# One token tile's merged activations turned by DMA transpose instead of TensorE, in a hybrid GLA/HGRN2 layer

## The chip, the cores and the metric

The kernel runs on one core of a Trainium2 chip. The metric is the device time of one execution in microseconds, as the median of several runs. The profile is of one further execution on the same kind of chip.

## The reference

One layer of a decoder trunk on 256 tokens of width 2048, all in float32. It has three parts: a SwiGLU half-step, a token mixer, and a second SwiGLU half-step. Each normalizes its input (RMSNorm) and normalizes its output again before it is added to the residual `h`. Cut to what matters here:

```python
f1 = swiglu(rms_norm(h, ...), ffn1_w_gate, ffn1_w_up, ffn1_w_down)      # D_FF = 5504
h = h + 0.5 * rms_norm(f1, ffn1_post_norm)
proj = rms_norm(h, mix_pre_norm) @ w_in                                 # eleven slices
o_gla, o_hgrn = ...                    # two causal gated recurrences, (256, 1024) each
merged = (sigmoid(z_gla + b0) * (o_gla @ w_branch_gla)
          + sigmoid(z_hgrn + b1) * (o_hgrn @ w_branch_hgrn))            # (256, 2048)
h = h + rms_norm(merged @ w_out, mix_post_norm)
f2 = swiglu(rms_norm(h, ...), ffn2_w_gate, ffn2_w_up, ffn2_w_down)
h = h + 0.5 * rms_norm(f2, ffn2_post_norm)
```

The change touches the way from `merged` to its product with `w_out`.

## The kernel before, in words

The 256 tokens are two token tiles (`NT` = 2) of 128 rows. A matrix product runs over row tiles of 128 input features and column blocks of 512 (`CB`). The weights are streamed from HBM in chunks of 128x1024 floats (`raw`). To keep float32 accuracy, every operand is split into a high part (`hi`, a copy by ScalarE, line 159) and a low part (`lo`, the difference, by VectorE, line 161). `mm3` (lines 165 to 167) then makes three matmuls: hi times hi, lo times hi, hi times lo. The split weights lie in a ring of five slots (`RING`); a new chunk can be split only when TensorE has finished with a slot. Some pairs of row tiles are done with seven block products in place of eight (`Blocks.seven`, lines 273 to 310); these need sums of weight blocks (`wsum`, split into `wsumh` and `wsuml`) and sums of activation blocks (`four_sums`).

A product's left operand must be turned, with features on the partitions. `to_T` (line 454) does this for a 128x512 block: four transposes on TensorE into a PSUM bank (`transpose4`, line 403), then ScalarE and VectorE split the bank into the `hi` and `lo` tiles, and `x[2][t]` is set to the number of row tiles that are ready. There is a second way, used by the feed-forward halves (`finish`, lines 678 to 689): `halved` (line 418) copies the block on ScalarE so that the low and the high 16 bits of all its floats lie apart, `turn` (line 426) issues a DMA transpose of the 16-bit data from ScalarE's queue, and `joined` (line 432) copies the turned halves on ScalarE back into floats.

The merge works like this. `ms[n][t]` holds the gated GLA branch and `szs[n][t]` the HGRN2 gate, for the column blocks n = 0 to 3. For each n, `gemm_block` multiplies by `w_branch_hgrn` (8 row tiles, 48 matmuls), and for each tile t `merge` (lines 1224 to 1232) is spawned: VectorE multiplies the product by the gate (line 1226) and adds the other branch (line 1227); then the block is turned by `to_T` into `mT`, and then the residual, which had been put away in DRAM (`away`), is loaded back over `ms` (line 1232, on ScalarE's queue).

After the merge `in_halves` multiplies `mT` by `w_out`, over two halves of the columns. The first half takes the row tiles in the order `OUT[0]`: 0, 1, the seven-product step of unit 1 (row tiles 2 and 3), 4, 5, that of unit 3 (row tiles 6 and 7), then 8 to 15. Column block n of the merge is row tiles 4n to 4n + 3. `sums_of(u)` makes the sums of unit u from `mT` of both tiles. `lhs_of` makes the program wait until the row tile that it wants has been written.

Order: small jobs are Python generators in a list (`Side`). Each `yield` ends a turn, and the gemm loops give all jobs a turn (`side.pump`) after every weight chunk, and twice in a seven-product step. This sets the order in the program. The framework then builds each engine's queue from the program and from its own estimate of when an instruction's inputs are ready; an engine works through its queue in that order. So the place of an instruction in the program is a rank and not a time: the trace has instructions of the merge and of the first sums well ahead of where the turns would put them.

Of the kernel before, what the change touches and what calls it, by code (L numbers as in the profile page):

```python
# [94 lines left out]
def kernel(ctx: ExitStack, tc: tile.TileContext, a: dict, out: bass.AP):  # L95
    nc = tc.nc
# [14 lines left out]
    def nm(s):  # L111
        uid[0] += 1
        return f"{s}_{uid[0]}"

    def ps_tile(s="ps"):
        return psum.tile([P, CB], F32, tag="ps", name=nm(s))
# [3 lines left out]
    away = [[dram.tile([P, CB], F32, name=f"away{t}_{n}") for n in range(4)] for t in range(NT)]  # L120
# [37 lines left out]
    def split_into(hi, lo, src):  # L158
        last[0] = nc.scalar.activation(hi, src, AF.Copy)  # L159
        with tc.issue_after(first_ops.pop().ins) if first_ops else nullcontext():  # L160
            nc.vector.tensor_tensor(lo, src, hi.bitcast(F32), op=ALU.subtract)  # L161
# [241 lines left out]
    def transpose4(dst_ps, src, n=4):  # L403
        for i in range(n):
            end = nc.tensor.transpose(dst_ps[:, i * P:(i + 1) * P], src[:, i * P:(i + 1) * P],  # L405
                                      ident)
        return end

    def tiles4(x):
        return x.rearrange("p (k c) -> p k c", c=P)  # L410

    def move(eng, dst, src):
        if eng is nc.scalar:
            nc.scalar.activation(dst, src, AF.Copy)
        else:
            eng.tensor_copy(dst, src)

    def halved(src, halves, eng=nc.scalar):

        w = src.shape[-1]  # L420
        halves = halves.bitcast(U16)[:, :2 * w]
        move(eng, halves.rearrange("p (h f) -> p h f", h=2),
             src.bitcast(U16).rearrange("p (f h) -> p h f", h=2))
        return halves

    def turn(halves):
        turned = work.tile([P, 8, P], U16, tag="tmp", name=nm("turned"), bufs=3)
        turned = turned[:, :halves.shape[-1] // P, :]
        nc.scalar.dma_start_transpose(turned, halves)
        return turned  # L430

    def joined(dst, turned, eng=nc.scalar):

        move(eng, dst.bitcast(U16).rearrange("p j (k h) -> p h j k", h=2),
             turned.rearrange("p (h j) k -> p h j k", h=2))

    def new_xT():
        x = [None] * NT, [None] * NT, [0] * NT
        for t in range(NT):
            alloc_xT(x, t)  # L440
        return x
# [12 lines left out]
    def to_T(x, t, n, src, col=None):  # L454


        ps = ps_tile()
        transpose4(ps, src)
        sl = slice(4 * n, 4 * n + 4)
        v = tiles4(ps)  # L460
        if col is not None:
            v = tiles4(work.tile([P, CB], F32, tag="tmp", name=nm("u"), bufs=3))
            nc.vector.tensor_tensor(v, tiles4(ps), col[:, sl].unsqueeze(2).broadcast_to([P, 4, P]),
                                    op=ALU.mult)
        split_into(x[0][t][:, sl, :], x[1][t][:, sl, :], v)
        x[2][t] = 4 * n + 4
# [295 lines left out]
    def mixer(x, rs, ready, following):  # L762
        xl = lhs_of(x)
        w_in = a["w_in"]
        with ExitStack() as mctx:
# [5 lines left out]
            def blk(s, dt=F32):  # L771
                return b2.tile([P, CB], dt, tag="b", name=nm(s), bufs=33)
# [449 lines left out]
            mT = new_xT()  # L1222

            def merge(t, n, b):
                s, m = szs[n][t], ms[n][t]
                nc.vector.tensor_tensor(s, b, s, op=ALU.mult)
                nc.vector.tensor_tensor(s, m, s, op=ALU.add)
                yield
                to_T(mT, t, n, s)
                for _ in range(6):  # L1230
                    yield
                nc.scalar.dma_start(m, away[t][n])

            side.until(lambda: not side.heavy)
            for n in range(4):
                b = gemm_block(a["w_branch_hgrn"], n * CB, CB, o_lhs("h"), nkt=8, ready=ready)
                ready = ()
                for t in range(NT):
                    side.spawn(merge(t, n, b[t]))
# [118 lines left out]
```

## Time and profile before

| | |
|---|---|
| median of 3 runs | 2058.8 us (2058.33 to 2060.32) |
| the profiled execution | 2058.24 us |
| its span, first to last instruction | 2056.4 us |
| mean granted TensorE clock | 0.999 |
| TensorE matmuls | 10319 |
| transposes of merged tiles, line 405 | 32, from 1253.1 to 1289.4 us |
| products with `w_branch_hgrn` | about 1239 to 1286 us |
| first half of the product with `w_out` | begins at 1285.87 us |
| ScalarE busy, whole span | 1317.2 us (64%) |
| DMA transposes (feed-forward halves) | 44 |

How to read it: a row of the trace has the start in microseconds, the duration, the engine, the line of the kernel, the operation, the output and input tiles, and at its end, in brackets, how long the engine had been idle before it and what ended this. `ACTq` and `SPq` are the queues' own instructions, such as the issue of a DMA. A row of waits has the waiting engine and line, what it waited for, the total in microseconds, the number of times and the longest. A row for a source line has three durations in nanoseconds: least, median and longest. The chain of waits goes back from the last instruction to what released it, and so on to the start.

### The profile page before, as it was taken

The numbers are of one execution on the slowest core, as the hardware profiler recorded it, in microseconds if no ns is written. First come the engines' busy times: TensorE is split into PE (matmuls) and PEld (weight loads), VectorE is DVE, ScalarE is ACT, GpSimd is POOL, SyncE is SP. The second block draws the span as 40 slices with busy tenths as digits, with TensorE's granted clock in tenths as the row PEclk, the third lists the DMA queues.
The fourth block names the chain that finished last, engine by engine and source line by source line (L and its number), as shares of the span: only waits on it lengthen the run. The fifth ranks groups of instructions, "written<-read, shape, count | busy, mean of one in ns | idle before, by whom it ended". The sixth has DMA issues, their size and how long they took to land.

```text
span 2056.4 us, 29076 instructions
## 1 busy us (share of the span) xinstructions
PE 2044.6 (99%) x10319; PEld 1699.8 (83%) x10319; DVE 1898.8 (92%) x2235; ACT 1317.2 (64%) x1726; POOL 42.4 (2%) x87
## 2 busy tenths in 40 slices
PE   9999999999999999999999999999999999999998
PEld 9888888888888888878888888888888888888886
DVE  8999999998999889989999898888999999999897
ACT  7666666666666576577655565556666666666663
POOL 1000000000000100000000000010000000000000
PEclk9999999999999999999999999999999999999999
DMA  8777677676757567556566566657767767776664
GB/s 258 223 215 230 203 217 224 212 225 206 233 182 235 157 199 224 158 177 191 167 201 191 180 219 217 219 156 211 235 203 220 223 214 208 224 236 201 205 194 146
DMA packets 247834, 423.51 MB, mean 206 GB/s; under 512 B 63668, under 2 KB 72055, under 8 KB 247688
## 3 DMA queue, kind: packets, MB, share of 16 engines
q1 hardware_dynamic: 196624, 401.80, 61.9%
q10 hardware_dynamic: 51064, 19.84, 4.6%
q8 instruction: 81, 1.33, 0.3%
q14 instruction: 65, 0.53, 0.1%
HBM read 406.11 MB, written 4.19 MB: 200 GB/s over the span
## 4 chain that ended last, share of the span: by engine, by line
PE 94%; DVE 3%; ACT 1%; issue 1%; DMA 1%; POOL 0%; DVEq 0%; POOLq 0%; ACTq 0%
PE c L165 22%; PE c L167 22%; PE c L166 22%; PE p L167 6%; PE p L165 6%; PE p L166 6%; PE mm L167 3%; PE mm L165 3%; PE mm L166 2%; PE ps L405 1%; DVE wlo L161 1%; DVE h L543 1%; PE ps L881 0%; DVE held L161 0%; DMA raw<-in_ffn_w_gate_dram 0%
## 5 line engine op out<-in xcount | busy, mean ns | idle before, releaser
L159 ACT ACTIVATE whi<-raw 128x1024 fp32r<-128x1024 f32 (+3 forms) x490 | 496.2, 1026 | 213.6 <-PE c L166 100.1
L161 DVE TENSOR_TENSOR wlo<-raw,whi 128x1024 fp32r<-128x1024 f32 (+3 forms) x490 | 573.7, 1184 | 44.1 <-ACT whi L159 42.2
L165 PE MATMUL c<-whi,xhi 128*128 128x512 f32 (+1 forms) x1358 | 529.2, 390 | 0.0
L166 PE MATMUL c<-whi,xlo 128*128 128x512 f32 (+1 forms) x1358 | 525.6, 387 | 0.0
L167 PE MATMUL c<-wlo,xhi 128*128 128x512 f32 (+1 forms) x1358 | 525.5, 387 | 0.0
L251 DVE TENSOR_TENSOR wlo<-raw,whi 128x1024 fp32r<-128x1024 f32 x264 | 314.4, 1219 | 20.4 <-ACT whi L290 15.4
L165 PEld LDWEIGHTS c<-whi,xhi 128*128 128x128 f32 x1358 | 254.9, 188 | 51.1 <-ACT xhi L502 0.6
L167 PEld LDWEIGHTS c<-wlo,xhi 128*128 128x128 f32 x1358 | 254.9, 188 | 50.8
L166 PEld LDWEIGHTS c<-whi,xlo 128*128 128x128 f32 x1358 | 255.0, 188 | 49.4
L290 ACT ACTIVATE whi<-raw 128x1024 fp32r<-128x1024 f32 x132 | 139.4, 1056 | 192.0 <-DVE raw L251 88.9
L251 DVE TENSOR_TENSOR wsuml<-wsum,wsumh 128x1536 fp32r<-128x1536 f32 x132 | 231.3, 1752 | 7.4 <-ACT wsumh L292 7.3
L165 PE MATMUL c<-whi,hkhi 128*128 128x512 f32 x542 | 210.9, 389 | 0.0
L167 PE MATMUL c<-wlo,hkhi 128*128 128x512 f32 x542 | 210.8, 389 | 0.0
L166 PE MATMUL c<-whi,hklo 128*128 128x512 f32 x542 | 210.8, 389 | 0.0
L288 ACT ACTIVATE wsumh<-wsum 128x1024 fp32r<-128x1024 f32 x132 | 139.0, 1053 | 87.9 <-DVE wsum L251 45.3
L286 ACT ACTIVATE whi<-raw 128x1024 fp32r<-128x1024 f32 x132 | 139.0, 1053 | 83.1 <-PE c L166 57.5
L251 DVE TENSOR_TENSOR wsum<-raw,raw 128x1024 f32<-128x1024 f32 x132 | 161.1, 1220 | 21.7 <-DMA raw<-in_ffn_w_down_dram 14.0
L167 PEld LDWEIGHTS c<-wlo,hkhi 128*128 128x128 f32 x542 | 101.7, 188 | 21.3
L166 PEld LDWEIGHTS c<-whi,hklo 128*128 128x128 f32 x542 | 101.7, 188 | 21.2
L165 PEld LDWEIGHTS c<-whi,hkhi 128*128 128x128 f32 x542 | 101.7, 188 | 20.9
L251 DVE TENSOR_TENSOR c<-c,psum 128x512 f32<-128x512 f32 x143 | 94.8, 693 | 11.5 <-PE c L167 11.2
L251 DVE TENSOR_TENSOR psum<-psum,p 128x512 f32<-128x512 f32 (+1 forms) x108 | 92.8, 859 | 2.3 <-ACT psum L318 0.6
(342 smaller groups left out, 3030.1 us busy)
## 6 DMA issues: line engine op xcount, KB each, us to landing
raw<-in_ffn_w_down_dram SPq DMA_DIRECT2D x120, 512.0 KB, 4.8
raw<-in_w_in_dram SPq DMA_DIRECT2D x104, 512.0 KB, 4.4
raw<-in_ffn_w_gate_dram SPq DMA_DIRECT2D x90, 512.0 KB, 4.8
raw<-in_ffn_w_up_dram SPq DMA_DIRECT2D x90, 512.0 KB, 3.7
raw<-in_ffn_w_gate_dram SPq DMA_DIRECT2D x140, 256.0 KB, 3.9
raw<-in_ffn_w_up_dram SPq DMA_DIRECT2D x140, 256.0 KB, 4.1
raw<-in_w_in_dram SPq DMA_DIRECT2D x128, 256.0 KB, 3.6
raw<-in_ffn_w_down_dram SPq DMA_DIRECT2D x104, 256.0 KB, 3.9
```

The lines of the kernel that those rows point to most:

```text
L159: last[0] = nc.scalar.activation(hi, src, AF.Copy)
L161: nc.vector.tensor_tensor(lo, src, hi.bitcast(F32), op=ALU.subtract)
L165: nc.tensor.matmul(ps, lhsT=xhi, rhs=whi, start=start, stop=False)
L166: nc.tensor.matmul(ps, lhsT=xlo, rhs=whi, start=False, stop=False)
L167: nc.tensor.matmul(ps, lhsT=xhi, rhs=wlo, start=False, stop=stop)
L251: return nc.vector.tensor_tensor(o, x, y, op=op)
L286: nc.scalar.activation(ahi, ra, AF.Copy)
L288: nc.scalar.activation(hi[:, 0:2, :], wsum[:, 0:2, :], AF.Copy)
L290: nc.scalar.activation(bhi, rb, AF.Copy)
L405: end = nc.tensor.transpose(dst_ps[:, i * P:(i + 1) * P], src[:, i * P:(i + 1) * P], ident)
L543: nc.vector.scalar_tensor_tensor(h[t][n], acc[t][n], r1, h[t][n], op0=ALU.mult, op1=ALU.add)
```

## The change

Only `merge` is touched. The second tile (t = 1) stays on TensorE, with twelve turns instead of six before its residual load. The first tile (t = 0) goes the feed-forward halves' way: the merged block's halves are copied by ScalarE into a new tile from the pool of 33 shared tiles, turned by DMA, and, eight turns later, joined by ScalarE over the merged block; a turn later they are split into `mT` from SBUF instead of from PSUM, `mT`'s count is set, and a turn after that the residual is loaded.

```diff
                 nc.vector.tensor_tensor(s, b, s, op=ALU.mult)
                 nc.vector.tensor_tensor(s, m, s, op=ALU.add)
                 yield
-                to_T(mT, t, n, s)
-                for _ in range(6):
+                if t:
+                    to_T(mT, t, n, s)
+                    for _ in range(12):
+                        yield
+                    nc.scalar.dma_start(m, away[t][n])
+                    return
+                halves = halved(s, blk("halves"))
+                yield
+                turned = turn(halves)
+                for _ in range(8):
                     yield
+                joined(tiles4(s), turned)
+                yield
+                sl = slice(4 * n, 4 * n + 4)
+                split_into(mT[0][t][:, sl, :], mT[1][t][:, sl, :], tiles4(s))
+                mT[2][t] = 4 * n + 4
+                yield
                 nc.scalar.dma_start(m, away[t][n])
```

The helpers that it calls:

```python
    def halved(src, halves, eng=nc.scalar):
        w = src.shape[-1]
        halves = halves.bitcast(U16)[:, :2 * w]
        move(eng, halves.rearrange("p (h f) -> p h f", h=2),
             src.bitcast(U16).rearrange("p (f h) -> p h f", h=2))
        return halves

    def turn(halves):
        turned = work.tile([P, 8, P], U16, tag="tmp", name=nm("turned"), bufs=3)
        turned = turned[:, :halves.shape[-1] // P, :]
        nc.scalar.dma_start_transpose(turned, halves)
        return turned

    def joined(dst, turned, eng=nc.scalar):
        move(eng, dst.bitcast(U16).rearrange("p j (k h) -> p h j k", h=2),
             turned.rearrange("p (h j) k -> p h j k", h=2))
```

## The prediction, made before the changed kernel ran

> **What bounds the kernel now.** I read the page's first part and its chain first, to see which engine sets the end; then TensorE's waits, to see whether anything ever holds it up; then the chain, the groups and the timeline of the stage from 1240 to 1320 us, where the changed code runs.
>
> ```profile
> PE 2044.6 (99%) x10319; PEld 1699.8 (83%) x10319; DVE 1898.8 (92%) x2235; ACT 1317.2 (64%) x1726; POOL 42.4 (2%) x87
> PE 94%; DVE 3%; ACT 1%; issue 1%; DMA 1%; POOL 0%; DVEq 0%; POOLq 0%; ACTq 0%
> PE ps L1298 <- POOL idle L1293: 1.3, 1, 1.3
> PE mm L167 <- DVE wlo L161: 0.8, 1, 0.8
> PE ps L941 <- ACT state L951: 0.4, 1, 0.4
> PE c L167 <- DVE held L161: 0.3, 1, 0.3
> PE ps L405 <- DVE h L543: 0.2, 1, 0.2
> ```
>
> TensorE (PE) works through 99% of the span and is 94% of the chain that ended last. All waits that the trace lists for it come to 1.3 + 0.8 + 0.4 + 0.3 + 0.2 = 3.0 us in 2056.4, none of them at the merge. So the end moves by what TensorE is given or spared, unless an edit makes it wait where it now does not. Two questions remain: how much of its time the removed transposes are, and whether the longer way of a tile by DMA can make it wait.
>
> **The removed transposes.** The 32 transposes of the merge stand in the chain of waits as six pieces, each long until the next matmul takes over:
>
> ```profile
> 1253.26 0.87 PE ps L405 x8
> 1265.04 0.44 PE ps L405 x4
> 1266.18 0.44 PE ps L405 x4
> 1276.85 0.44 PE ps L405 x4
> 1278.43 0.53 PE ps L405 x4
> 1288.75 0.87 PE ps L405 x8
> L405 PE MATMUL ps<-ident,sz x32: 270/272/329, 1253.1 to 1289.4; 128*128 128x128 f32 x32
> ```
>
> A piece of 8 is both tiles' four transposes of one column block (blocks 0 and 3), a piece of 4 is one tile's. Together they are 0.87 + 0.44 + 0.44 + 0.44 + 0.53 + 0.87 = 3.59 us. The change keeps the second tile's, four pieces of 4: 4 x 0.44 = 1.76 us. Spared: 3.59 - 1.76 = **1.83 us**, or 0.11 us for each of 16 transposes. The row of the transposes gives 0.272 us for each, but that is an instruction's own duration, and neighbours overlap; by it the sum would be 16 x 0.272 = 4.35 us. I take the chain's pieces, which are what the next matmul waits for, and keep 4.35 as the far end.
>
> The Trainium skill (TensorE: Matmul & The Clock Gate, Part 4: PE-mode transpose) gives about 275 ns for a transpose inside a kernel; an estimate from that page would be 16 x 0.275 = 4.4 us. The trace agrees on the duration, at 0.272 us, and not on what it costs the stream.
>
> **What is added to ScalarE (ACT) and its queue.** The feed-forward halves turn tiles of this size by the same helpers, so the trace has the prices:
>
> ```profile
> L414 ACT ACTIVATE halves<-silu x44: 825/1043/1060, 44.5 to 1825.5; 128x1024 uint16<-128x1024 uint16 x40, 128x768 uint16<-128x768 uint16 x4
> L414 ACT ACTIVATE hT<-turned x44: 1048/1360/1384, 51.6 to 1841.1; 128x1024 uint16<-128x1024 uint16 x40, 128x768 uint16<-128x768 uint16 x4
> L429 ACTq DMA_TRANSPOSE turned<-halves x44: 1233/1250/2367, 45.4 to 1826.9; - x44
>   ACT hT L414: 10.9, 10
> DMA to landing us min/median/max: 3.1/4.8/7.9
> 1254.08 1.06 ACT L159 ACTIVATE xhi<-ps 128x512 fp32r<-128x512 f32 x2
> 1260.41 0.62 ACT L159 ACTIVATE ms<-sums 128x512 fp32r<-128x512 f32 x1
> 1255.36 1.28 DVE L161 TENSOR_TENSOR xlo<-ps,xhi 128x512 fp32r<-128x512 f32 x2
> 1262.29 0.68 DVE L161 TENSOR_TENSOR ms<-sums,ms 128x512 fp32r<-128x512 f32 x1
> 1277.00:1289.00 12.00, 12.00 (x59) 9.81 (x58) 11.96 (x17) 6.05 (x8) 0.00 (x0) 1.00 0.67 196
> 1297.00:1307.00 10.00, 10.00 (x46) 8.28 (x45) 9.47 (x9) 6.96 (x9) 0.00 (x0) 1.00 0.65 206
> ```
>
> Per block of the first tile: copying the halves 1.04 us, issuing the DMA transpose 1.25 us, joining 1.36 us, 3.65 us in all and 14.6 us for four blocks. The split itself stays: its ScalarE half took 0.53 us from PSUM (1.06 for two) and 0.62 from SBUF on a tile of the same size, its VectorE (DVE) half 0.64 and 0.68, so it costs at most 0.1 us more. In the first window (after the length: TensorE, weight load, VectorE, ScalarE) ScalarE is busy 6.05 us of 12, about one block's pace, which leaves 6 us for 3.65. I cost this at nothing, because ScalarE fits it into idle time. The transposes' bytes go beside the weights, and DMA is 0.65 to 0.67 busy there (the last column but one); TensorE never waited for a weight in this stage, so I cost them at nothing too.
>
> The cover is the ring of split weights. The wait rows below show ScalarE idle until TensorE lets a ring slot go:
>
> ```profile
> 1253.12 1.06 ACT L159 ACTIVATE whi<-raw 128x1024 fp32r<-128x1024 f32 x1 [1.66 <-PE mm L166]
> 1292.22 1.06 ACT L286 ACTIVATE whi<-raw 128x1024 fp32r<-128x1024 f32 x1 [1.58 <-PE c L166]
> 1293.45 0.63 ACT L159 ACTIVATE ms<-sums 128x512 fp32r<-128x512 f32 x1 [0.16 <-DVE sums L214]
> 1296.96 1.06 ACT L290 ACTIVATE whi<-raw 128x1024 fp32r<-128x1024 f32 x1 [2.88 <-PE c L166]
> 1297.93 1.04 ACT L288 ACTIVATE wsumh<-wsum 128x1024 fp32r<-128x1024 f32 x1
> 1298.88 0.62 ACT L292 ACTIVATE wsumh<-wsum 128x512 fp32r<-128x512 f32 x1
> 1299.71 1.75 DVE L251 TENSOR_TENSOR wsuml<-wsum,wsumh 128x1536 fp32r<-128x1536 f32 x1
> 1305.57 0.39 PE L167 MATMUL p<-wsuml,ms 128*128 128x512 f32 x1
> ```
>
> A step of the gemm is 12 matmuls of 0.227 us, 2.72 us, and the ring has five slots: a weight split when a slot comes free is read four steps later, 10.9 us, less 1.06 for the copy and about 1.2 for the subtraction. So in blocks 0 to 2 ScalarE may be late by some 8 us before TensorE stands. The thin place is the seven-product step of unit 3: its summed weights' low part ends at 1299.71 + 1.75 = 1301.46 and is read at 1305.57, 4.1 us of cover, and block 3's new work falls just ahead of it.
>
> **The wait that is added.** Joining must wait for the DMA, and whatever is queued on ScalarE behind the join waits too. Block 3's merged tile stands like this:
>
> ```profile
> 1286.45 0.69 DVE L1227 TENSOR_TENSOR sz<-h,sz 128x512 f32<-128x512 f32 x1
> 1251.90 0.94 ACTq L1232 DMA_DIRECT2D h<-away  x2
> L1232 ACTq DMA_DIRECT2D h<-away x8: 326/327/337, 1251.9 to 1289.7; - x8
> DMA to landing us min/median/max: 2.6/3.1/4.0
> 1318.04 0.39 PE L165 MATMUL c<-whi,xhi 128*128 128x512 f32 x1
> ```
>
> It is ready at 1287.14; halves until 1288.2, then the DMA is issued. With the median landing of 4.8 us the join can start at 1293.0, and join plus split copy take 1.36 + 0.62, until about 1295.0. ScalarE was idle for 2.88 us until 1296.96, so it is back in time. TensorE first reads the block at row tile 12, at 1318.04, over 20 us later; blocks 1 and 2 are made 10 us later than now and are read 20 us after that or more. With the longest landing, 7.9 us, the join ends the idle time late: ScalarE is free at 1288.2 + 7.9 + 1.98 = 1298.1. If the join is queued ahead of the row at 1292.22, five copies wait behind it (1.06 + 0.63 + 1.06 + 1.04 + 0.62 = 4.4 us, to 1302.5), and VectorE ends at 1304.25. TensorE, 1.83 us early, wants it at 1303.74: a stand of 0.5 us. A gain at this wait is excluded, as TensorE waits for nothing here now. So the wait costs 0 to 0.5 us; I take 0, since the median landing clears it, and ten waits of 10.9 us in total on such joins in the feed-forward halves held up TensorE nowhere.
>
> **The later residual loads.** They are moved in the program past the first tile's split, and from six to twelve turns for the second tile. The row at 1251.90 shows that turns do not hold them: the first pair went out as VectorE finished with the tile, six turns early. Eight issues of 0.33 us on ScalarE's queue remain, landing in 2.6 to 4.0 us, and the residual is first added at about 1366. Moving them costs nothing, unless they land ahead of a transpose in the same queue (below).
>
> **Sum.** -1.83 + 0 + 0 + 0 = -1.83 us. The profiled execution took 2058.24 us, 1.84 us beyond its span of 2056.4, and would become 2056.4; the median of the three runs, 2058.8, would become **2057.0 us**. That is 0.09% less; about 0.2%, 4.1 us, is what a measurement of this kernel can tell from no change.
>
> **Rivals.**
>
> *Whole durations.* If each transpose holds TensorE for its row's 0.272 us, 4.35 us go, and the time is 2054.4. For it speaks only the row; against it the pieces of 0.44 us for four. Chance 0.06.
>
> *A landing behind the residual loads.* If block 3's transpose stands in its queue behind two residual loads of 3.1 us, it lands after 4.8 + 6.2 = 11.0 us. By the working above, the stand is the landing less 7.4 us: 3.6 us, and the time is 2058.8 - 1.8 + 3.6 = 2060.6, slower than before. It decides from a landing of 7.4 us; from 9.2 us the change loses, from 13.3 us it loses more than 0.2%. For it: the loads and the transpose share ScalarE's queue, and the loads do go out as soon as the tile is free. Against it: no transpose among 44 took over 7.9 us. Chance 0.14, half of it (several blocks caught, or a landing beyond 13.3 us) over 0.2%.
>
> The Trainium skill (VectorE: DVE Perf Modes, Rules for kernel authors) speaks against the change: transpose a 128x128 block on TensorE where PSUM will do as the destination, else by the DMA's crossbar. No run here sets the two side by side; the rule would have this rival's sign.
>
> *Given back.* Behind the mixer the chain leaves TensorE:
>
> ```profile
> 1348.65 6.46 DMA raw<-in_ffn_w_gate_dram
> 1366.49 2.08 DVE h L543 x3
> ```
>
> If this stretch follows the order of loads and VectorE's queue and not TensorE's earlier finish, the 1.83 us are waited out there: 2058.8. For it: the two rows; against it: both are released by work that TensorE ends. Chance 0.15.
>
> **How the numbers follow.** Forecast 0.62, given back 0.15, late landing 0.14, whole durations 0.06, and 0.03 for another order of instructions on the engines, whose sign I can't tell. Within 0.2% are the forecast, the giving back and half of the late landings: 0.62 + 0.15 + 0.07 = 0.84. Of the last 0.03 I give 0.01 to faster and 0.02 to slower, and one more hundredth of the forecast to slower: faster 0.07, same 0.83, slower 0.10. The range runs from whole durations, 2054.4, to the late landing, 2060.6.
>
> **What would show it.** Right: the merge's transposes down to 16, in pieces of 4 and 0.44 us; ScalarE up by about 10 us (2.4 us of copies a block), with four more transposes landing in 3 to 8 us; TensorE's waits still near 3 us. Wrong: a wait of TensorE for `wsuml`, `wlo` or the second tile's merged blocks between 1285 and 1320 us, a landing above 9 us, or new TensorE waits between 1345 and 1380 us.

## The result, and the profile after

The changed kernel takes 2065.92 us (median of 7 runs, 2064.67 to 2067.53) where the kernel before, run beside it, takes 2058.7: a ratio of 1.0037, 95% interval [1.0028, 1.0046]. It is 7.2 us slower where 1.8 us faster was forecast, and lies above the range. The profiled execution took 2064.67 us with a span of 2062.9, 6.5 us more than before.

The page's first part, and the row of the second DMA queue (packets, MB, share of 16 engines; 51064 packets, 19.84 MB and 4.6% before):

```profile
PE 2044.8 (99%) x10303; PEld 1698.8 (82%) x10303; DVE 1898.2 (92%) x2235; ACT 1325.8 (64%) x1734; POOL 42.3 (2%) x87
q10 hardware_dynamic: 55288, 20.89, 5.2%
```

TensorE has 16 instructions fewer, as foreseen, and is busy just as long; ScalarE has gained 8.6 us. The page's chain of waits covers only 29% of the span here (it breaks off before it reaches the merge), so it says nothing of the change. TensorE's waits can:

```profile
PE ps L405 <- DVE sz L1227: 4.9, 3, 4.4
PE ps L1312 <- POOL idle L1307: 1.3, 1, 1.3
PE p L167 <- DVE wsuml L251: 1.3, 2, 0.7
PE mm L167 <- DVE wlo L161: 0.8, 1, 0.8
```

The first row is new: the transposes that stayed on TensorE wait for the merge (line 1227) that makes their input. So is the third, which comes late, in the second SwiGLU half.

To place the loss without the scatter of the rest, I use two marks on GpSimd that TensorE's progress sets: a fill long before the merge (line 909), and the first sum of squares of the product with `w_out` (line 474). Before, then after:

```profile
869.74 0.53 POOL L909 MEMSET sc<- 128x512 f32 x1 [42.51 <-PE ps L405]
1330.97 0.19 POOL L474 TENSOR_TENSOR v<-ss 128x1 f32<-128x1 f32 x1 [122.74 <-ACT sq L485]
```

```profile
868.97 0.53 POOL L909 MEMSET sc<- 128x512 f32 x1 [42.53 <-PE ps L405]
1335.42 0.19 POOL L474 TENSOR_TENSOR v<-ss 128x1 f32<-128x1 f32 x1 [127.97 <-ACT sq L485]
```

The stretch between them, which I call the stage, took 461.23 us before and 466.45 after: 5.22 us more, where 1.83 less was forecast. In the two kernels below whose merge leaves TensorE and the DMA as they were it took 461.25 and 461.22, so a difference of a few tenths of a us means something between executions like these. It is one execution of each kernel, though. The executions of a kernel with transposes by DMA in the merge lie up to 6.8 us apart (2056.34 to 2063.12 us in one of those below), so a stage figure belongs to the execution that was profiled, and the medians stand beside it.

What happened in it can be read engine by engine, after the change. First ScalarE and its queue:

```profile
1251.13 1.06 ACT L414 ACTIVATE halves<-sz 128x1024 uint16<-128x1024 uint16 x1 [0.44 <-DVE sz L1227]
1251.14 0.34 ACTq L1246 DMA_DIRECT2D h<-away  x1
1252.22 1.27 ACTq L429 DMA_TRANSPOSE turned<-halves  x1
1261.37 1.36 ACT L414 ACTIVATE sz<-turned 128x1024 uint16<-128x1024 uint16 x1 [4.79 <-DMA turned<-halves]
1262.77 0.63 ACT L159 ACTIVATE xhi<-sz 128x512 fp32r<-128x512 f32 x1
```

Block 0's halves are copied, a residual load and then the transpose go out, and ScalarE stands 4.79 us at the join. The four landings of the merge's transposes:

```profile
DMA to landing us min/median/max: 3.1/5.0/9.1
```

This one is the 9.1. VectorE:

```profile
1256.61 1.23 DVE L161 TENSOR_TENSOR wlo<-raw,whi 128x1024 fp32r<-128x1024 f32 x1
1263.43 0.69 DVE L161 TENSOR_TENSOR xlo<-sz,xhi 128x512 fp32r<-128x512 f32 x1 [5.60 <-ACT xhi L159]
1264.50 1.22 DVE L161 TENSOR_TENSOR wlo<-raw,whi 128x1024 fp32r<-128x1024 f32 x1
1265.64 1.28 DVE L1226 TENSOR_TENSOR sz<-mm,sz 128x512 f32<-128x512 f32 x2
1266.84 1.28 DVE L1227 TENSOR_TENSOR sz<-h,sz 128x512 f32<-128x512 f32 x2
```

Its next instruction is the low part of the joined tile, so it stands 5.60 us; the merge of block 1 (lines 1226 and 1227) is queued behind that. TensorE:

```profile
1263.48 0.39 PE L167 MATMUL mm<-wlo,oT 128*128 128x512 f32 x1
1268.26 0.85 PE L405 MATMUL ps<-ident,sz 128*128 128x128 f32 x4 [4.40 <-DVE sz L1227]
1270.19 0.63 PE L165 MATMUL mm<-whi,oT 128*128 128x512 f32 x1
1270.62 0.63 PE L166 MATMUL mm<-whi,oT 128*128 128x512 f32 x1
1273.07 0.39 PE L165 MATMUL mm<-whi,oT 128*128 128x512 f32 x1
1273.30 0.39 PE L166 MATMUL mm<-whi,oT 128*128 128x512 f32 x1
```

It stands 4.40 us for the second tile's merged block, which has nothing to do with the transposed tile; it only comes after it in two queues. Then matmuls start 0.43 us apart (1270.19 to 1270.62) instead of 0.23 (1273.07 to 1273.30). The windows show why (the last three columns are the granted clock, the DMA share and GB/s):

```profile
1268.00:1270.00 2.00, 1.74 (x7) 1.58 (x8) 2.00 (x5) 2.00 (x3) 0.00 (x0) 0.63 0.35 141
1270.00:1272.00 2.00, 2.00 (x6) 1.52 (x6) 1.61 (x3) 0.03 (x1) 0.00 (x0) 0.52 0.83 201
1272.00:1274.00 2.00, 2.00 (x11) 1.64 (x10) 0.00 (x0) 0.96 (x1) 0.00 (x0) 1.00 1.21 268
```

The granted clock was about half for some 3.4 us. Eight starts about 0.2 us late are another 1.6 us. The Trainium skill (TensorE: Matmul & The Clock Gate, Why this matters for your kernels) asks for no idle gap of TensorE above about 3 us between bursts of matmuls; the trace agrees, with a gap of 4.40 us. It doesn't follow that a shorter gap is safe: in two kernels below the clock fell to half after gaps of 1.90 and 1.95 us.

The sum: -1.83 + 4.40 + 0.46 (the two shorter stands of the first row of waits) + 1.6 = +4.6 of the stage's +5.22. Most of the span's other differences lie outside: 0.77 us less ahead of the stage, and 1.96 us more in the second SwiGLU half (line 474's marks at 1377.60 and 1943.97, against 1373.25 and 1937.66 before).

### The profile page after: what moved, and what is told of

Its sections match the earlier page's. It is cut to its first block, busy times and chain, and to the rows that moved or that the text cites. A ratio compares the mean times of both kernels' runs of the same rounds, so it can differ in the third digit from the quotient of the medians.

```text
span 2062.9 us, 29049 instructions
## 1 busy us (share of the span) xinstructions
PE 2044.8 (99%) x10303; PEld 1698.8 (82%) x10303; DVE 1898.2 (92%) x2235; ACT 1325.8 (64%) x1734; POOL 42.3 (2%) x87
## 5 line engine op out<-in xcount | busy, mean ns | idle before, releaser
L251 DVE TENSOR_TENSOR wsum<-raw 128x512 f32<-128x512 f32 x132 | 91.1, 690 | 3.7
```

The source lines that it names most:

```text
L251: return nc.vector.tensor_tensor(o, x, y, op=op)
```

## The experiments

Three theories stood at first. **Theory Q** (queues): the join stands too early in ScalarE's queue; what waits behind it on ScalarE and VectorE holds up the next block's merge, and TensorE, whose queue has that block's transposes next, stands. **Theory R** (residual loads): the loss is the long landing, made by residual loads ahead of the transposes; without them the joins would not matter. **Theory W** (work): the added copies and transfers cost the time by themselves. `tc.issue_after(last[0].ins)` keeps an instruction behind the latest high-part copy (lines 159 and 292) that ScalarE has in the program; "held" means that. Edits are shown against the changed kernel, except in the kernels with unread transposes or with the copies alone, where they are against the kernel before. Stage differences are against before's 461.23 us; times are medians, with the kernel before run beside them.

### The join held

```diff
-                joined(tiles4(s), turned)
+                with tc.issue_after(last[0].ins):
+                    joined(tiles4(s), turned)
```

> The join of each turned block may not be queued on ScalarE before the weight split that stands next to it in the program (eight turns after the transpose is issued); nothing else changes. Theory Q (queue order): the loss is one in-order wait, ScalarE standing 4.8 us at block 0's join, VectorE 5.6 us behind it, TensorE 4.4 us behind that and then some matmuls at a lower clock; with the join later in the queue all of it goes, TensorE's waits fall to about 3 us and the time to about 2057 (2056 to 2059). Theory W (work): the copies and the DMA traffic as such starve the weight stream; then they still do, and the time stays at 2064 to 2066.

2056.99 us against 2059.49, ratio 0.9989 [0.9979, 0.9998]; stage -1.38. TensorE has no wait in the merge. The join, the landings, and block 1's merge on VectorE:

```profile
1266.35 1.38 ACT L414 ACTIVATE sz<-turned 128x1024 uint16<-128x1024 uint16 x1
```

```profile
DMA to landing us min/median/max: 3.4/8.3/10.9
```

```profile
1260.48 1.40 DVE L1226 TENSOR_TENSOR sz<-mm,sz 128x512 f32<-128x512 f32 x2
```

The landings are longer than in the changed kernel, yet ScalarE waits for none of them at a join (no bracket here). The merge of block 1 starts at 1260.48 instead of 1265.64, 5.16 us earlier, and a stand of 4.40 is gone: the merge had a slack of about 0.8 us. For Q, against R and W.

### Block 0 alone by DMA

```diff
-                if t:
+                if t or n:
```

> Only block 0 of the first tile goes by DMA, blocks 1 to 3 of it stay on TensorE. Theory Q: the whole stand belongs to block 0, so nearly all of the loss stays: 2063 to 2066. Theory W: a quarter of the added work remains, so about a quarter of the 7 us: 2060 to 2061.

2064.48 us against 2059.49, ratio 1.0023 [1.0013, 1.0033]; stage +5.89. One transpose, landing after 9.9 us, makes a stand of ScalarE of 5.59 us, of VectorE of 6.40 and of TensorE of 4.60. The profiled execution was the slowest of nine (2067.94 us); by the medians block 0 alone costs 5.0 us of the 7.2. So the first block does most of the harm.

### Only the residual loads held

```diff
-                    nc.scalar.dma_start(m, away[t][n])
+                    with tc.issue_after(last[0].ins):
+                        nc.scalar.dma_start(m, away[t][n])
```

(Both loads; the joins as in the changed kernel.)

> Each residual load may not be queued before the weight split next to it in the program, so the loads stay out of the 10 us around block 0's transpose; the joins are queued as early as in the changed kernel. Theory R (the residual loads in the same queue make the landing 9.1 us): the landing falls to about 5 us, ScalarE's stand from 4.8 to about 1, TensorE's from 4.4 to under 1, the time to 2057 to 2060. If the transpose is slow beside the weights alone, the landing stays at 8 to 9 us and the time at 2063 to 2066.

2065.86 us against 2059.49, ratio 1.0028 [1.0017, 1.0039]; stage +5.29. The join of block 0 and TensorE's stands:

```profile
1257.61 1.37 ACT L414 ACTIVATE sz<-turned 128x1024 uint16<-128x1024 uint16 x1 [2.44 <-DMA turned<-halves]
```

```profile
1267.55 0.63 PE L405 MATMUL ps<-ident,sz 128*128 128x128 f32 x4 [2.92 <-DVE sz L1227]
1283.86 0.63 PE L405 MATMUL ps<-ident,sz 128*128 128x128 f32 x4 [2.27 <-DVE sz L1227]
```

Half of R holds: without a residual load ahead of it, the first transpose lands 3.8 us sooner (the join starts 5.3 us after the issue at 1252.30, against 9.1). The other half falls: three joins still wait (2.44, 3.22 and 0.38 us), TensorE now stands at two blocks, and the time is the same. Ahead of the second stand VectorE also waits 1.27 us for a weight load.

### The second tile's transposes held

```diff
-                    to_T(mT, t, n, s)
-                    for _ in range(12):
+                    for _ in range(3):
+                        yield
+                    with tc.issue_after(lastmm[0].ins):
+                        to_T(mT, t, n, s)
+                    for _ in range(9):
```

(`lastmm[0]` is the latest hi times lo matmul of `mm3`, line 167; the line that keeps it isn't shown. The joins stay early.)

> The second tile's four transposes of each block may not be queued on TensorE before the matmul that stands next to them three turns later in the program; the early join stays, so ScalarE and VectorE still stand behind block 0's landing. Theory Q: TensorE has matmuls to do while the merge is late, the ring of weights covers the rest, and TensorE's stand at these transposes falls from 4.9 us to under 1: 2057 to 2060. Theory W, or weights that come late behind the same stand of VectorE: TensorE waits for the low parts of the weights instead, 2062 to 2066.

2064.0 us against 2059.49, ratio 1.0026 [1.0016, 1.0036]; stage +5.33. The wait for a merged block is gone, and this stands in its place:

```profile
1303.27 0.50 PE L167 MATMUL p<-wlo,xhi 128*128 128x512 f32 x1 [1.95 <-DVE wlo L251]
1306.75 1.12 PE L405 MATMUL ps<-ident,sz 128*128 128x128 f32 x4 [1.31 <-ACT psum L318]
```

VectorE still stood 5.51 us for block 0. Moving TensorE's reader back doesn't give that time back: VectorE has little idle time to catch up in (in this kernel it is busy 36.56 of the 40 us from 1263, and in the kernel before 36.32), and I read the two stands as this debt coming due, at the seven-product step of unit 3. That place, which the prediction named as the thin one, is the second to break. The run doesn't separate this from what the later transposes do to VectorE's queue by themselves.

### The join held two turns less

```diff
-                for _ in range(8):
+                for _ in range(6):
                     yield
-                joined(tiles4(s), turned)
+                with tc.issue_after(last[0].ins):
+                    joined(tiles4(s), turned)
```

> A smaller dose of the first experiment: the join is held six turns behind the transpose instead of eight, which puts block 0's join one weight split (about 2.7 us) later in ScalarE's queue than the changed kernel has it, and still ahead of block 1's halves. Theory Q: with a landing near 1261 us ScalarE stands about 2 us instead of 4.8, TensorE about 1 to 2 us, and the time lies between, 2058 to 2061. If only joins behind block 1's merge help, it stays at 2064 to 2066.

2061.8 us against 2058.71, ratio 1.0013 [1.0004, 1.0023]; stage +0.78. ScalarE stands 1.9 us at joins and TensorE 1.30 and 0.93 us for merged blocks. Between "as early as the scheduler likes" and "eight turns" the loss follows the join's place, as Q has it.

### The transposed data unread

Both tiles go by TensorE, and what is computed is unchanged; the first tile's halves are also copied, turned by DMA and joined late into a block that nobody reads.

```diff
+                if not t:
+                    halves = halved(s, blk("halves"))
                 to_T(mT, t, n, s)
-                for _ in range(6):
+                yield
+                if not t:
+                    turned = turn(halves)
+                for _ in range(8):
+                    yield
+                if not t:
+                    joined(tiles4(blk("spare")), turned)
+                for _ in range(3):
                     yield
```

> The 32 transposes of the merge stay on TensorE and feed the product; besides, the first tile's halves are copied, turned by DMA and joined into a spare tile that nobody reads, so all the added work of ScalarE and all the added DMA traffic are there, with the joins late in the queue. Theory Q: no one waits for it, 2058 to 2060 (no change within 0.1%). Theory W: the added work itself costs, 2063 or more.

2066.29 us against 2058.71, ratio 1.0034 [1.0021, 1.0047]; stage +5.44. A clear miss of Q as it stood, and the time that W had given: ScalarE stands at no join, and the loss is there. VectorE and TensorE:

```profile
1278.73 1.22 DVE L251 TENSOR_TENSOR wsum<-raw,raw 128x1024 f32<-128x1024 f32 x1 [4.79 <-DMA raw<-in_w_out_dram]
```

```profile
1280.61 1.11 PE L405 MATMUL ps<-ident,sz 128*128 128x128 f32 x4 [3.96 <-DVE sz L1227]
```

In VectorE's queue a sum of two weight chunks stands between the two steps of block 2's merge (lines 1226 and 1227), and it waits for a weight load that is late. Theory Q was widened: *any* instruction that waits on a DMA ahead of a merge in ScalarE's or VectorE's queue passes the wait to TensorE, and the transposes make the DMAs late. The two kernels with the copies alone and with the loads held, below, test this.

### Only the later residual loads, and both tiles by DMA

Two ends of the change. First, both tiles on TensorE with twelve turns before the load.

```diff
-                if t:
+                if True:
```

> The part of the change on the residual loads alone: both tiles on TensorE, twelve turns instead of six before the loads. Every theory: the loads go out as soon as the merged tile is done, as before, so 2058 to 2060 and no change; a loss here would mean that the loads' place carries part of it.

2059.21 us against 2058.71, ratio 1.0004 [0.9994, 1.0013]; stage +0.02. The later loads alone cost nothing.

Then both tiles by DMA with the joins held.

```diff
-                if t:
-                    to_T(mT, t, n, s)
...
-                    return
...
-                joined(tiles4(s), turned)
+                with tc.issue_after(last[0].ins):
+                    joined(tiles4(s), turned)
```

> Both tiles go by DMA, all joins held eight turns as in the first experiment; TensorE has no transposes in the merge. Theory Q with the spared pieces as the only gain: 3.59 us less than before, about 2055.2 (2054 to 2057). If ScalarE, now with about 20 us more copies, or the DMA queue, with eight transposes, becomes late for the weights, TensorE waits for the low parts and the time is 2058 or more.

2056.69 us against 2058.71, ratio 0.9992 [0.9983, 1.0002], which doesn't exclude no change; stage -2.88, and no wait of TensorE in it. The stage's figure is 0.09 us for each of 32 transposes, and -1.38 in the first experiment is 0.09 for each of 16; the prediction had 0.11.

### ScalarE's copies without the transposes

Both tiles by TensorE; the halves are copied apart and put back into the block, and nothing goes by DMA.

```diff
+                if not t:
+                    spare = halved(s, blk("halves"))
                 to_T(mT, t, n, s)
-                for _ in range(6):
+                for _ in range(8):
+                    yield
+                if not t:
+                    joined(tiles4(s), spare.rearrange("p (j k) -> p j k", k=P))
+                for _ in range(4):
                     yield
```

> Both tiles are turned by TensorE, as before; block by block of the first tile ScalarE makes the change's two extra copies (the halves, and the halves put back into the block), nothing goes by DMA, and the residual loads come late. VectorE's order is the one in which the last run stood 4.79 us: a weight sum ahead of a merge. If the transposes' traffic made that stand, as theory Q now says, the weight sum waits under 1 us, no transpose of TensorE waits over 1 us for a merged block, and the time is 2058 to 2061 us. If ScalarE's 14.6 us of extra copies were the cost, the time stays at 2063 us or above without any transpose by DMA.

2059.13 us against 2058.44, ratio 1.0005 [0.9996, 1.0014]; stage -0.01. The copies are free, and the weight sum waits for nothing in the same order of instructions. What remains is the traffic. (The 14.6 us above count the issues of the transposes too; the copies alone are 4 x 2.40 = 9.6 us.)

### The unread transposes, with the residual loads held

The kernel whose transposed data nobody reads, with one edit more:

```diff
-                nc.scalar.dma_start(m, away[t][n])
+                with tc.issue_after(last[0].ins):
+                    nc.scalar.dma_start(m, away[t][n])
```

> As the run in which TensorE turns both tiles and the first tile is also turned by DMA into blocks that nobody reads, but the residual loads, which are the size of a transpose, are issued as late as TensorE's weight splits allow, behind the transposes. If transposes and residual loads together crowd the weight loads, the weight sum's stand of 4.79 us falls under 2 us and the time to 2058 to 2061 us. If the four transposes alone do it, the stand stays at 3.5 us or more and the time at 2064 to 2067 us.

2061.25 us against 2058.44, ratio 1.0014 [1.0005, 1.0023]; stage +3.23. The weight sum's stand:

```profile
1276.60 1.23 DVE L251 TENSOR_TENSOR wsum<-raw,raw 128x1024 f32<-128x1024 f32 x1 [3.18 <-DMA raw<-in_w_out_dram]
```

It fell between the two expectations: transposes and residual loads both crowd the weights. Part of the difference between the two stages is the clock, which fell to 0.50 after the first kernel's stand of 3.96 us and stayed at 1.00 after this one's 2.35. The 10 us from 1263 to 1273 show one transpose by itself, since the first residual loads come later. The two queues, and the weight chunks issued there (KB each, median us to landing), in this kernel:

```profile
q10 hardware_dynamic: 1054, 0.26, 53.3%
q1 hardware_dynamic: 389, 1.19, 49.9%
raw<-in_w_out_dram SPq DMA_DIRECT2D x4, 256.0 KB, 6.5
```

and in the kernel with the copies alone, where the second queue has two residual loads:

```profile
q1 hardware_dynamic: 743, 1.84, 56.6%
q10 hardware_dynamic: 288, 0.52, 15.7%
raw<-in_w_out_dram SPq DMA_DIRECT2D x4, 256.0 KB, 4.3
```

The packets of one transpose of 0.26 MB, about a thousand small ones, took 53.3% of the 16 engines' time over 10 us; those of two residual loads with twice its bytes took 15.7%. The weights' bytes fell from 1.84 to 1.19 MB. The Trainium skill (Advanced Engine Details and Errata, X-Bar Transpose) has transpose DMAs as fast as regular ones; in this stretch the trace says otherwise, by about seven times the packet time for a byte. In the window from 1252 to 1262 of the same kernel a transpose took 15.3% for as many bytes, about twice the loads' time for a byte, so this is no fixed price.

### Join and loads held

The edits of the first and the third experiment together:

```diff
-                joined(tiles4(s), turned)
+                with tc.issue_after(last[0].ins):
+                    joined(tiles4(s), turned)
...
-                nc.scalar.dma_start(m, away[t][n])
+                with tc.issue_after(last[0].ins):
+                    nc.scalar.dma_start(m, away[t][n])
```

> The changed kernel with the joins held until some eight of TensorE's weight splits after the transpose was issued, and the residual loads held too. Theory Q: no wait of TensorE for a merged block, landings of 4 to 8 us, 2056 to 2057.5 us, as with the joins held alone or a little below. If the residual loads, now later, come too late for the next layer's merges, TensorE gets a wait for psum to be copied or for a merged block after 1320 us, and the time is 2059 us or more.

2057.57 us against 2058.44, ratio 0.9996 [0.9987, 1.0005]. The median is 0.9 us lower, which is not clear of no change. The profiled execution was the slowest of eleven, 2063.12 us, with the stage at +2.22: VectorE's weight sum stood 1.7 us for its load, and TensorE 1.90 us for block 3's merged tile. Right after, matmuls start 0.43 us apart from 1292.10 to 1295.09, and the granted clock from 1292 to 1294 is 0.52. So -1.38 for the spared transposes, 1.90, and about 1.6 for the clock make +2.1 of the +2.22. The other executions have no profile; their spread (2056.34 to 2059.79 us) suggests that such a stand comes and goes between executions of one kernel. Holding the loads is no better than holding the join alone.

### The joins early, only the split of the joined tile held

```diff
-                split_into(mT[0][t][:, sl, :], mT[1][t][:, sl, :], tiles4(s))
+                with tc.issue_after(last[0].ins):
+                    split_into(mT[0][t][:, sl, :], mT[1][t][:, sl, :], tiles4(s))
```

> The changed kernel with the joins where they are, early in ScalarE's queue, and only the first tile's splits held, so that on VectorE the low-part subtraction of the joined tile (the row that stood 5.60 us) stands behind the next block's merge. If that subtraction alone passes the join's wait to the merge, VectorE no longer stands over 2 us before the merge, TensorE waits for no merged block, and the time is 2056 to 2058 us. If it is ScalarE's stand as such (theory Q in its wider form: a weight copy queued behind the join, and its subtraction queued ahead of the merge, pass the wait on just as well), VectorE stands 3 to 5 us for a weight's high part, TensorE waits 1.5 to 4.5 us for a merged block, some 1.2 us less than in the changed kernel, and the time is 2060.5 to 2065 us.

2070.3 us against 2060.19, ratio 1.0052 [1.0035, 1.0069]; stage +7.05. VectorE, then TensorE:

```profile
1264.63 1.22 DVE L161 TENSOR_TENSOR wlo<-raw,whi 128x1024 fp32r<-128x1024 f32 x1 [6.17 <-ACT whi L159]
1265.77 1.28 DVE L1226 TENSOR_TENSOR sz<-mm,sz 128x512 f32<-128x512 f32 x2
```

```profile
1268.39 1.09 PE L405 MATMUL ps<-ident,sz 128*128 128x128 f32 x4 [3.92 <-DVE sz L1227]
1284.53 0.63 PE L405 MATMUL ps<-ident,sz 128*128 128x128 f32 x4 [2.03 <-DVE sz L1227]
```

The joined tile's low part is out of VectorE's way, and a weight's low part takes its place, because the weight's copy is behind the join on ScalarE. So it is ScalarE's stand as such, not one unlucky neighbour. The time is above what either theory expected: block 2's merge is caught as well, since ScalarE stood at all four joins (9.2 us). Outside the stage, another 2.8 us more than before lie in the second SwiGLU half; they aren't explained here.

## Why the prediction was wrong

**The step that failed** is the cover of the added wait: "So in blocks 0 to 2 ScalarE may be late by some 8 us before TensorE stands." ScalarE was late by 4.79 us and TensorE stood 4.40. The weights were covered: TensorE waited for none of them in this merge. But I followed only the weights from ScalarE to TensorE, and worked the wait out only for block 3. VectorE's queue also holds the next block's merge, behind the subtractions that follow ScalarE; and TensorE's queue has the second tile's transposes of that merge about one weight chunk into the next block. That path had a slack of 0.8 us, not 8. The prediction's own window row from 1277 to 1289 us has VectorE busy 11.96 of 12 us; I read only ScalarE's 6.05 out of it. It is the case that I set aside as covered, block 0, that does most of the harm (5.0 us by the medians with one block alone).

Of the signs that I had named as wrong, two came: TensorE waiting for the second tile's merged blocks, though the long wait ends at 1268 us and only one of 0.28 us falls between 1285 and 1320, and a landing above 9 us.

**The transfers at no cost** were the second failure: "TensorE never waited for a weight in this stage, so I cost them at nothing too". With the data unread and no join waited for, the same transposes cost 5.44 us in the stage (3.23 with the residual loads held); the same copies without them cost nothing. A DMA share of 0.65 to 0.67 did not mean room for them. In the changed kernel itself, though, this path hardly counted. There too the weight sum stands between the two steps of block 2's merge, and it waited 0.39 us, with TensorE's stand of 0.18 us behind it:

```profile
1279.07 1.23 DVE L251 TENSOR_TENSOR wsum<-raw,raw 128x1024 f32<-128x1024 f32 x1 [0.39 <-DMA raw<-in_w_out_dram]
```

With the joins held, the sum stands behind that merge, and four transposes cost nothing. So in the changed kernel the traffic acted mainly through block 0's long landing.

**The lower clock** after a long stand, 1.6 us, was in no term.

**What was right.** ScalarE's extra copies are free (-0.01). The later loads alone are free (+0.02). Beside the transposes they lengthen block 0's landing by 3.8 us, though holding them back did not change that kernel's time. The transposes spared are worth what the chain's pieces said, a little less: 1.38 us in the stage, 0.09 us each against 0.11. Their row's duration would have made it 4.35, and that rival is out. With 1.38 in place of 1.83, the sum of the result section comes to 5.1 of the stage's 5.22 us.

**The rivals.** The late landing had the right sign and half the mechanism: a residual load ahead of the transpose, a landing of 9.1 us, above the 7.9 that no other had passed. Its place (block 3) and its price (landing less 7.4 us, so 1.7) were wrong, and with the join held a landing of 10.9 us cost nothing. Giving back doesn't show in the changed kernel: from line 474's mark at 1330.97 to the next stage's at 1373.25 took 42.28 us before and 42.18 after, and 41.53 with the join held. It isn't excluded either. With both tiles by DMA, where TensorE ends the stage earliest, that stretch took 43.65 us and TensorE waited 1.56 us in it for a weight's high part; but three kernels with a longer stage than before's took 43.24 to 43.61 there too, so single profiles don't decide it.

**Left open.** The 1.9 us past the mixer: in after a transpose of the second SwiGLU half landed after 7.6 us, its join waited 4.0 us, and TensorE waited 1.3 us for `wsuml`. So the ten waits that "held up TensorE nowhere" may have been near the edge too. But the kernel with only the later loads has a wait of 0.7 us there and 565.88 us in that stretch, the one with only the copies none and 564.22, before 564.41, after 566.37. So I don't charge it to the merge. Nor is it settled why one transpose lands in 3.1 us and another in 11.1.

## What to carry to other kernels

When a wait is added to an in-order engine, list what is queued behind it, then what is queued behind *those* on the next engine, and take the smallest slack on any such path, not the depth of the buffer that the first one feeds. Place the reader of a DMA by the longest landing, not the median: holding the join alone turned 7.2 us slower into 2.5 us faster than the kernel before (ratio 0.9989 [0.9979, 0.9998]). And ask of a new transfer what it delays, since a mean share of the DMA engines says little about the next load that somebody stands waiting for.

## What the runs showed of the hardware

After stands of TensorE of 2.9 us or more (2.92, 3.92, 3.96, 4.40, 4.60 us) the granted clock fell to about half. Shorter stands went both ways: after 1.90 us (join and loads held) and 1.95 us (second tile's transposes held) it fell too, after 2.03, 2.27 and 2.35 us it stayed at 1.00. By the clock in windows of 1 us, the half clock lasted about 3.4 us in five of these seven kernels and 6.8 us in two (the split held, and the second tile's transposes held).

The transposes in the merge landed after 3.1 to 11.1 us over all these kernels. The DMA engines' share passed 1.0 in windows in which they moved less: from 1263 to 1273 us it was 1.04 at 147 GB/s with a transpose and the weights, and 0.73 at 239 GB/s with two residual loads and the weights.
